# Layer 0 of a two-layer diffusion trunk: tokens and RMS factor first, adaLN scale and shift streamed together, q from the finished input

## The chip, the core and the metric

The kernel runs on one core of a Trainium2 chip. Its engines are TensorE (PE, with its weight loads shown apart as PEld), VectorE (DVE), ScalarE (ACT), GpSimd (POOL) and SyncE (SP), which issues most of the loads. The metric is the time of one execution on the device in microseconds; the median of three runs stands for the kernel. All data are float32; the large products split each operand into a high and a low part of the type fp32r.

## The reference, cut to what matters

Layer 0 takes 384 tokens (128 of a prompt, 256 of a sample) of 2048 features. The two groups have their own condition vector.

```python
def rms_norm(x, g):
    y = x * lax.rsqrt(jnp.mean(x * x, axis=-1, keepdims=True) + EPS)
    return y * g

def adaln(cond, w_mod, b_mod):
    m = jax.nn.silu(cond) @ w_mod + b_mod
    shift, scale, gate = jnp.split(m, 3, axis=-1)
    return shift[:, None, :], scale[:, None, :], gate[:, None, :]

# in reference(), for each layer and each of the two groups
h = rms_norm(x, g) * (1.0 + scale) + shift
proj = h @ w_in          # ga, gb, gate_a, q, k, v, gate_b for layer 0
```

After that, layer 0 runs a conformer branch (a 31-tap convolution over `ga * sigmoid(gb)`, layer norm, SiLU, a gate) beside attention with normed q and k, projects the joined result with `w_out`, multiplies by `gate` and adds it to x. Layer 1 does the like with other branches, and a final RMS norm ends it.

## The kernel before

Features lie on the 128 partitions, in 16 chunks of 128; the tokens lie along the free axis (`xT` is 128 x 16 x 384). The normed and modulated input of a layer is held as `hhi` and `hlo`, each weight tile as `whi` (a cast on ScalarE, line 261) and `wlo` (what the cast left over, on VectorE, line 262). A product is three matmuls, hi by hi, hi by lo and lo by hi. `proj_feat` gives features by tokens (line 354, 384 columns), `proj_tok` and `q_unit` give tokens by features (lines 333 and 571, 512 columns). There are two buffers' worth of room in few places only: three `whi`, three `wlo`, seven raw weight tiles of 512 KB, four slots of 1 MB for the adaLN weights (`ring`), four buffers of the tag `wk` for rows of 384.

The adaLN vectors are products of one row pair with a weight of 2048 x 2048 per part (scale, shift, gate). `gemv_block` loads such a weight in tiles (line 139 holds its matmuls, which write four 32-row strips of one bank); `mod_part` then copies the bank on ScalarE (line 143), transposes it on TensorE (line 172), sums it on VectorE (158), adds the bias (160) and, for the scale, multiplies by the norm's gain (163). With `widths` the scale of layer 0 comes in blocks of 256, 256, 512, 512 and 512 features, that is 2, 2, 4, 4 and 4 chunks.

The first stage of before works so. The blocks of scale are loaded, and with each block the tokens of the same chunks. `make_h` multiplies x by scale only: neither the RMS factor nor the shift is in `hhi` and `hlo` yet. `q_unit` projects q of such a chunk at once. The squares for the RMS factor are summed beside that (`square_sum`, ScalarE and GpSimd), so that the factor `rs0` is there when q is evacuated from PSUM, and is multiplied in there (line 507). The shift is loaded later, four tiles ahead of each quarter of the k and v projection (`shifted`); it makes the finished `hhi` and `hlo` that all later projections read. q misses the shift's share so far. It is added in a bias pass: `wq0` is loaded a second time in 16 half-megabyte tiles, the shift (`sst`) is multiplied with it by `gemv_block`, a selector matmul (line 634) spreads the two rows over the tokens, and VectorE adds the result to q (line 637).

The order of the instructions is made by a scheduler from priorities: `first()` gives the stage's code the highest, `later()` a low one; within an engine the order is fixed at build time and each engine then runs its list in order. SP's list of loads is held in program order by `sync_load`. Work without a place of its own, the remaining adaLN parts and the bias pass, hangs in `gemv_q`; `pump` takes `bg["rate"]` of its tiles after each unit of a projection (R0 until attention, RA after it, RB from the layer norm on).

In the rows, `gv` is the bank of the adaLN products and of the bias pass, `ring` and `raw` are weight tiles, `q`, `pt` and `pf` the banks of q, of the token projections (k and v first) and of the feature projections, `cst` the condition, `gs` the copied bank, `mod` the finished vector, `area` and `mix` scratch rooms for other adaLN parts on VectorE.

Of the kernel before, what the change touches and what calls it, by code (L numbers as in the profile page):

```python
# [19 lines left out]
P = 128  # L20
D = 2048
# [21 lines left out]
R0 = 1.7  # L43
SHIFT_AT = (7, 9, 11)
RA = 1.35
RB = 1.1
# [5 lines left out]
def trunk(ctx: ExitStack, tc: tile.TileContext, d: dict, o: dict):  # L52
# [69 lines left out]
    def gemv_block(w, f0, nf, stat, done):  # L122
# [3 lines left out]
        def unit(u):  # L126
            if u == 0:
                st["ps"] = ps_gv.tile([P, 512], F32, tag="gv", name="gv")
# [12 lines left out]
            if nk * (u + 1) == KC:  # L141
                gs = tmp.tile([P, 512], F32, tag="gs", name="gs", bufs=1)
                nc.scalar.copy(gs[:, :nf], ps[:, :nf])
                done(gs, ps)
# [20 lines left out]
    def mod_part(layer, part, widths=(512, 512, 512, 512), f0=0):  # L165
# [10 lines left out]
        for nf in widths:  # L176
            units += gemv_block(d[f"mod_w{layer}"][4 * part + f0 // 512], f0 % 512, nf, lambda k: cst[:, 2 * k:2 * k + 32],
                                lambda gs, ps, f0=f0, nf=nf: consume(f0, nf, gs, ps))
            f0 += nf
# [319 lines left out]
    def qkv_evacs(v, nat, rs=None):  # L499
        def ev_q(q):  # L500
            def ev(t, ps):
                dst = nat[t][:, 4 * q:4 * q + 4, :]
                src = ps.rearrange("p (h c) -> p h c", h=4)
                if rs is None:
                    nc.scalar.copy(dst, src)
                else:
                    nc.scalar.activation(dst, src, AF.Copy, scale=rs[:, t:t + 1])
# [65 lines left out]

    widths = (256, 256, 512, 512, 512)
    scale_q = mod_part(0, 1, widths)
    pq = [[acc("q0") for t in range(NT)], [acc("q1"), acc("q1"), aux("q1")]]
    av, square = square_sum()
    k0 = 0
    for j, nf in enumerate(widths):
        n = nf // P  # L580
        with first():
            for _ in range(2048 // (2048 // nf * P)):
                scale_q.pop(0)()
            sync_load(xT[:, k0:k0 + n, :], d["xT"][:, k0:k0 + n, :])
            for k in range(k0, k0 + n):
                make_h(0, k)
        last = j == len(widths) - 1
        if last:
            for k in range(k0, KC):
                square(k)  # L590
        for k in range(k0, k0 + n):
            q_unit(k)
            if not last:
                square(k)
            elif k == k0 + 1:
                rs0 = rstd_cols([av], D, "rs0")
                rb0 = rstd_rows(rs0, "rb0")
# [5 lines left out]
    eq0, eq1, ekv = qkv_evacs(v, nat, rs0)  # L603
# [7 lines left out]
    shift_q = mod_part(0, 0)  # L611

    def shifted(u):
        with first():
            for _ in range(4):
                shift_q.pop(0)()
        for k in range(4 * u, 4 * u + 4):
            h = tmp.tile([P, T], F32, tag="wk", bufs=4, name="h32")
            scale_norm(0, h, k, rb0)
            shift_split(0, h, k)  # L620
    proj_tok(d["wkv0"][0], ekv, before=shifted)
# [4 lines left out]
    selb = spare[:, :256].rearrange("p (g c) -> p g c", g=2)  # L626
    side_load(selb, d["selb"])
    sst = spare[:, 1280:1792].rearrange("p (k c) -> p k c", c=32)
    nc.gpsimd.memset(sst, 0.0)
    nc.gpsimd.tensor_copy(sst[:, :, 0:2], mods[0, 0])  # L630
# [343 lines left out]
```

## Time and profile before

| | |
|---|---|
| median of 3 runs | 1300.25 us (1298.58 to 1300.34) |
| span of the profiled execution | 1295.9 us |
| PE busy | 1267.4 us, 98% of the span, 7000 records |
| DVE busy | 882.0 us, 68% |
| ACT busy | 544.5 us, 42% |
| POOL busy | 142.2 us, 11% |
| DMA | 252.76 MB, mean 195 GB/s |

The profiled execution's own time is read as its span, from the first to the last instruction; the runs' times are a little above it. A float32 product (adaLN, transposes of some kinds, attention) appears as more than one record for each instruction of the program, so counts of records and of instructions differ there. Times in the rows are microseconds from the start of the span unless marked ns. A matmul's end is modelled, so TensorE's busy share says less than the number of matmuls in a stretch.

### The profile page before, as it was taken

To read this page: it belongs to the slowest core of one execution; us is meant where nothing else is said; L and a number is where in the kernel's file an instruction comes from. 1 tells how busy PE (TensorE), PEld (TensorE's weight loads), DVE (VectorE), ACT (ScalarE), POOL (GpSimd) and SP (SyncE) were. 2 spreads that over 40 slices of the span, in tenths; PEclk is the share of its full clock that TensorE was granted. 3 is DMA by queue.
4 is the path that set the end of the run, shared out by engine and by line. 5 is a ranking of instruction groups with operands and counts; after the bars stand their busy time and mean duration, and the time that the engine had idled before them with its cause. 6 is when DMAs were issued, how large, how long until landed. Compare 5 with 4: busy or idle time off the path is not lost.

```text
span 1295.9 us, 18150 instructions
## 1 busy us (share of the span) xinstructions
PE 1267.4 (98%) x7000; PEld 1123.1 (87%) x7000; DVE 882.0 (68%) x1464; ACT 544.5 (42%) x941; POOL 142.2 (11%) x162
## 2 busy tenths in 40 slices
PE   6999999999999999999999999999999999999997
PEld 4566687888887888999999988899999999999997
DVE  2245627899999979989976932454544689996443
ACT  3344433644556645432363633344444422343332
POOL 0210100210000042122220000000000011111110
PEclk9999999999999999999999999999999999999998
DMA  9988867688654566676644444433333577764412
GB/s 364 403 309 313 300 185 258 232 307 295 226 166 160 196 221 218 209 225 217 199 135 130 121 128 130 123 118 109 98 99 103 185 231 229 252 194 146 123 50 98
DMA packets 71222, 252.76 MB, mean 195 GB/s; under 512 B 7456, under 2 KB 11808, under 8 KB 67552
## 3 DMA queue, kind: packets, MB, share of 16 engines
q1 hardware_dynamic: 59920, 211.90, 48.9%
q0 software_dynamic: 11072, 39.60, 9.8%
q8 instruction: 55, 0.90, 0.3%
q14 instruction: 31, 0.25, 0.1%
q10 hardware_dynamic: 144, 0.10, 0.0%
HBM read 247.91 MB, written 3.67 MB: 194 GB/s over the span
## 4 chain that ended last, share of the span: by engine, by line
PE 85%; DMA 5%; DVE 5%; issue 3%; POOL 1%; ACT 1%; SPq 0%; DVEq 0%; POOLq 0%; ACTq 0%
PE pf L354 57%; PE pt L333 10%; PE q L571 6%; PE gv L139 5%; DMA area<-in_mod_w 3%; DVE area L197 2%; PE s_ps L470 2%; PE o_ps L495 2%; DVE wlo L262 1%; DMA raw<-in_wf 1%; PE pT_ps L491 1%; DMA ring<-in_mod_w 1%; PE gv L172 1%; POOL lvar L718 1%; PE y_ps L862 1%
## 5 line engine op out<-in xcount | busy, mean ns | idle before, releaser
L354 PE MATMUL pf<-hhi,whi 128*128 128x384 f32 (+1 forms) x1664 | 569.2, 342 | 0.7 <-ACT whi L261 0.7
L354 PE MATMUL pf<-hlo,whi 128*128 128x384 f32 (+1 forms) x1664 | 569.7, 342 | 0.0
L354 PE MATMUL pf<-hhi,wlo 128*128 128x384 f32 (+1 forms) x1664 | 567.2, 343 | 1.7 <-DVE wlo L262 1.7
L262 DVE TENSOR_TENSOR wlo<-raw,whi 128x1024 fp32r<-128x1024 f32 x256 | 314.8, 1230 | 294.3 <-ACT whi L261 288.9
L261 ACT CAST whi<-raw 128x1024 fp32r<-128x1024 f32 x256 | 268.3, 1049 | 466.3 <-PE pf L354 242.5
L354 PEld LDWEIGHTS pf<-hhi,whi 128*128 128x128 f32 x1664 | 313.1, 188 | 24.0 <-issue 14.2
L354 PEld LDWEIGHTS pf<-hhi,wlo 128*128 128x128 f32 x1664 | 313.3, 188 | 9.8 <-issue 3.2
L354 PEld LDWEIGHTS pf<-hlo,whi 128*128 128x128 f32 x1664 | 313.6, 188 | 5.3 <-issue 2.9
L197 DVE SCALAR_TENSOR_TENSOR area<-area,cst 128x512 f32<-128x512 f32 x240 | 177.8, 777 | 14.7 <-DMA area<-in_mod_w 14.5
L659 DVE SCALAR_TENSOR_TENSOR cv<-apad,cw,cv 128x399 f32<-128x399 f32 x240 | 140.6, 635 | 1.1 <-ACT cv L657 0.8
L91 POOL DMA_DIRECT2D area<-in_mod_w x64 | 34.7, 542 | 424.0 <-DVE area L197 222.0
L333 PE MATMUL pt<-wlo,hhi 128*128 128x512 f32 x192 | 75.8, 395 | 0.0
L254 POOL TENSOR_TENSOR sacc<-sacc,sqf 128x384 f32<-128x384 f32 x43 | 55.2, 1284 | 186.9 <-ACT sqf L253 185.1
L333 PE MATMUL pt<-whi,hhi 128*128 128x512 f32 x192 | 75.7, 397 | 0.0
L333 PE MATMUL pt<-whi,hlo 128*128 128x512 f32 x192 | 75.0, 396 | 0.0
L333 PEld LDWEIGHTS pt<-whi,hhi 128*128 128x128 f32 x192 | 36.0, 188 | 12.4 <-ACT hhi L280 2.5
L571 PE MATMUL q<-whi,hhi 128*128 128x512 f32 x96 | 41.1, 428 | 4.4 <-ACT hhi L267 4.4
L478 ACT ACTIVATE pr<-s_ps,nm 128x384 f32<-128x384 f32 (+1 forms) x48 | 24.4, 509 | 49.7 <-DVE nm L477 34.7
L333 PEld LDWEIGHTS pt<-whi,hlo 128*128 128x128 f32 x192 | 36.0, 188 | 10.1 <-issue 0.8
L333 PEld LDWEIGHTS pt<-wlo,hhi 128*128 128x128 f32 x192 | 36.1, 188 | 9.0 <-issue 0.8
L139 PE MATMUL gv<-ring,cst 128*32 128x512 f32 (+1 forms) x288 | 35.8, 582 | 8.2 <-DMA ring<-in_mod_w 7.6
L571 PE MATMUL q<-wlo,hhi 128*128 128x512 f32 x96 | 40.5, 422 | 0.0
(171 smaller groups left out, 991.8 us busy)
## 6 DMA issues: line engine op xcount, KB each, us to landing
raw<-in_wf SPq DMA_DIRECT2D x144, 512.0 KB, 4.5
ring<-in_mod_w SPq DMA_DIRECT2D x32, 1024.0 KB, 7.5
area<-in_mod_w POOLq DMA_DIRECT2D x64, 512.0 KB, 4.6
raw<-in_w_out SPq DMA_DIRECT2D x64, 512.0 KB, 4.4
raw<-in_mod_w SPq DMA_DIRECT2D x56, 512.0 KB, 5.6
raw<-in_wq SPq DMA_DIRECT2D x32, 512.0 KB, 8.8
raw<-in_wt SPq DMA_DIRECT2D x24, 512.0 KB, 3.6
raw<-in_wkv SPq DMA_DIRECT2D x8, 512.0 KB, 7.8
```

What stands on the lines that cost most here:

```text
L91: ins = nc.gpsimd.dma_start(dst, src).ins
L139: nc.tensor.matmul(ps[32 * g:32 * g + 32, :nf], lhsT=stat(k), rhs=raw[:, i % raw.shape[1], :], start=(k < 4), stop=(k >= KC - 4))
L197: nc.vector.scalar_tensor_tensor(av[:, g], raw[:, i], cst[:, 2 * k + g:2 * k + g + 1], av[:, g], ALU.mult, ALU.add)
L254: nc.gpsimd.tensor_tensor(av, av, s, ALU.add)
L261: nc.scalar.copy(dst_hi, src)
L262: order["split"] = nc.vector.tensor_tensor(dst_lo, src, dst_hi.bitcast(F32), ALU.subtract).ins
L333: nc.tensor.matmul(pp[t], lhsT=x[:, k, tt], rhs=y[:, i, :], start=(k == 0 and n == 0), stop=(k == KC - 1 and n == 2))
L354: ins = nc.tensor.matmul(pp[j][:, :n], lhsT=x[:, i, fj], rhs=y[:, k, :n], start=(begin and k % 8 == 0 and m == 0), stop=(end and k % 8 == ...
L470: nc.tensor.matmul(ps, lhsT=mix[:, h0 + h, t * P:(t + 1) * P], rhs=kT[:, kv, c0:c0 + nk * P], start=True, stop=True)
L495: nc.tensor.matmul(po, lhsT=v[:, slots[j], kv * HD:(kv + 1) * HD], rhs=pT[:, j, :], start=(j == 0), stop=(j == nk - 1))
L571: nc.tensor.matmul(pq[b][t], lhsT=x[:, k, tt], rhs=y[:, 0, 512 * b:512 * b + 512], start=(k == 0 and n == 0), stop=(k == KC - 1 and n == 2))
L659: nc.vector.scalar_tensor_tensor(st["o"], apad[:, c, j:j + CVW], cw[:, c, j:j + 1], st["o"], ALU.mult, ALU.add)
```

## The change

All tokens are loaded first, in four loads. `norm_sum` squares them on ScalarE and adds on VectorE; the RMS factor by token (`rb0`) follows at once. Then scale and shift of a block are loaded one after the other through the same four slots, the shift with a PSUM bank (`aux`) and a copy room of its own. `norm_h` makes the finished input of a chunk: x by the factor on GpSimd, scale and shift in one VectorE operation per group, then the split. q is projected from that. The bias pass with its second load of `wq0`, the selector table and `add_bias` is gone, and so are `make_h` and `shifted` from layer 0; q is evacuated by a plain copy. The three rates of the background work are 1.0, 1.0 and 0.8 in place of 1.7, 1.35 and 1.1.

```diff
-R0 = 1.7
+R0 = 1.0
-RA = 1.35
-RB = 1.1
+RA = 1.0
+RB = 0.8
...
+    def norm_sum():
+        av = tmp.tile([P, T], F32, tag="sacc", name="sacc", bufs=1)
+        for c in range(4):
+            sync_load(xT[:, 4 * c:4 * c + 4, :], d["xT"][:, 4 * c:4 * c + 4, :])
+            for k in range(4 * c, 4 * c + 4):
+                if k == 0:
+                    nc.scalar.activation(av, xT[:, k, :], AF.Square)
+                else:
+                    s = tmp.tile([P, T], F32, tag="wk", bufs=4, name="sqx")
+                    nc.scalar.activation(s, xT[:, k, :], AF.Square)
+                    nc.vector.tensor_tensor(av, av, s, ALU.add)
+        return av
+
+    def norm_h(k):
+        h = tmp.tile([P, T], F32, tag="wk", bufs=4, name="h32")
+        nc.gpsimd.tensor_tensor(h, xT[:, k, :], rb0, ALU.mult)
+        for g, c0, c1 in GROUPS:
+            nc.vector.tensor_scalar(h[:, c0:c1], h[:, c0:c1], mods[0, 1][:, k, g:g + 1], mods[0, 0][:, k, g:g + 1],
+                                    ALU.mult, ALU.add)
+        split(hhi[:, k, :T], hlo[:, k, :T], h)
+
     widths = (256, 256, 512, 512, 512)
     scale_q = mod_part(0, 1, widths)
+    shift_q = mod_part(0, 0, widths, bank=lambda: aux("gv_shift"),
+                       row=lambda: big.tile([P, 512], F32, tag="att", name="gs_shift", bufs=3))
     pq = [[acc("q0") for t in range(NT)], [acc("q1"), acc("q1"), aux("q1")]]
-    av, square = square_sum()
+    with first():
+        rb0 = rstd_rows(rstd_cols([norm_sum()], D, "rs0"), "rb0")
     k0 = 0
-    for j, nf in enumerate(widths):
+    for nf in widths:
         n = nf // P
         with first():
-            for _ in range(2048 // (2048 // nf * P)):
-                scale_q.pop(0)()
-            sync_load(xT[:, k0:k0 + n, :], d["xT"][:, k0:k0 + n, :])
+            for q in (scale_q, shift_q):
+                for _ in range(n):
+                    q.pop(0)()
             for k in range(k0, k0 + n):
-                make_h(0, k)
...
+                norm_h(k)
         for k in range(k0, k0 + n):
             q_unit(k)
...
-    shift_q = mod_part(0, 0)
-
-    def shifted(u):
...
-    proj_tok(d["wkv0"][0], ekv, before=shifted)
+    proj_tok(d["wkv0"][0], ekv)
...
-    def add_bias(b, gs, pb):
-        for g, ts in ((0, (0,)), (1, (1, 2))):
-            nc.tensor.matmul(pb, lhsT=selb[:, g, :], rhs=gs, start=True, stop=True)
-            for t in ts:
-                x = nat[t][:, 4 * b:4 * b + 4, :]
-                nc.vector.tensor_tensor(x, x, pb.rearrange("p (h c) -> p h c", h=4), ALU.add)
-    bias_q = [f for b in range(2) for f in
-              gemv_block(d["wq0"][0], 512 * b, 512, lambda k: sst[:, k, :], lambda gs, ps, b=b: add_bias(b, gs, ps))]
...
-    gemv_q.extend(bias_q + mod_part(0, 2) + mod_part(1, 1, (512,) * 3))
+    gemv_q.extend(mod_part(0, 2) + mod_part(1, 1, (512,) * 3))
```

On TensorE before, at the end of the fourth block of scale, the four transposes of the copied bank stand among the q matmuls of the third block (`q_101` and its like are the six banks of q; the last adaLN product stands 22 rows further up):

```order
L571 MATMUL q_101<-whi,hlo 128x512
L571 MATMUL q_102<-whi,hhi 128x512
L172 MATMUL gv<-ident,gs 128x128 x4
L571 MATMUL q_102<-wlo,hhi 128x512
L571 MATMUL q_102<-whi,hlo 128x512
L571 MATMUL q_103<-whi,hhi 128x512
```

On TensorE now, at the end of the second block (`gv_shift` is the shift's bank, `gs_shift` its copy):

```order
L572 MATMUL q_106<-wlo,hhi 128x512
L572 MATMUL q_106<-whi,hlo 128x512
L145 MATMUL gv<-ring,cst 32x512 x4
L145 MATMUL gv_shift<-ring,cst 32x512 x4
L178 MATMUL gv<-ident,gs 128x128 x4
L145 MATMUL gv_shift<-ring,cst 32x512 x4
L145 MATMUL gv_shift<-ring_98,cst 32x512 x4
L145 MATMUL gv_shift<-ring,cst 32x512 x4
L178 MATMUL gv_shift<-ident,gs_shift 128x128 x4
L572 MATMUL q_101<-whi,hhi 128x512
```

The q matmuls of the second block are all ahead of the last adaLN products and of both sets of transposes; the next row of q belongs to the third block. The fourth and the fifth block end in the same way, with the last tile of shift, its transposes, and then q of the next block.

On VectorE before, at the third block, between the sum of the scale's transposes and the first `hlo` of that block:

```order
L158 TENSOR_REDUCE mod_99<-gv 128x8
L160 TENSOR_TENSOR mod_99<-mod_99,vecs 128x8
L262 TENSOR_TENSOR wlo<-raw,whi 128x1024
L163 SCALAR_TENSOR_TENSOR mod_99<-mod_99,vecs 128x8
L262 TENSOR_TENSOR wlo<-raw,whi 128x1024
L268 SCALAR_TENSOR_TENSOR hlo<-xT,mod_99,hhi 128x128
```

On VectorE now, at the same place (`h_456` is the first chunk's x times the factor):

```order
L164 TENSOR_REDUCE mod_99<-gv 128x8
L166 TENSOR_TENSOR mod_99<-mod_99,vecs 128x8
L169 SCALAR_TENSOR_TENSOR mod_99<-mod_99,vecs 128x8
L268 TENSOR_TENSOR wlo<-raw,whi 128x1024 x2
L164 TENSOR_REDUCE mod_100<-gv_shift 128x8
L166 TENSOR_TENSOR mod_100<-mod_100,vecs 128x8
L268 TENSOR_TENSOR wlo<-raw,whi 128x1024
L592 TENSOR_SCALAR h_456<-h_456,mod_99,mod_100 128x128
L592 TENSOR_SCALAR h_456<-h_456,mod_99,mod_100 128x256
```

Two weight splits stand ahead of the shift's sum and one behind it; `hhi` of the chunk, on ScalarE, can only follow the last two rows. On ScalarE the copy into `gs_shift` has one weight cast ahead of it there:

```order
L149 COPY gs<-gv 128x512
L267 CAST whi<-raw 128x1024
L149 COPY gs_shift<-gv_shift 128x512
L267 CAST whi<-raw 128x1024 x2
L267 CAST hhi<-h_456 128x384
```

## Rows read from the trace of the kernel before

**Rows 1.** The page, part 1: busy us, share of the span, records of TensorE.

```profile
PE 1267.4 (98%) x7000; PEld 1123.1 (87%) x7000; DVE 882.0 (68%) x1464; ACT 544.5 (42%) x941; POOL 142.2 (11%) x162
```

**Rows 2.** Windows of 20 us: busy us (records) by engine, PEclk, DMA share, GB/s.

```profile
core 0: us, PE busy (x) PEld busy (x) DVE busy (x) ACT busy (x) POOL busy (x), PEclk, DMA share, GB/s
0.00:20.00 20.00, 9.76 (x48) 5.68 (x49) 4.19 (x12) 6.40 (x12) 1.20 (x5) 1.00 0.96 329
...
280.00:300.00 20.00, 20.00 (x125) 17.35 (x123) 20.00 (x38) 7.60 (x14) 1.25 (x3) 1.00 0.87 296
...
540.00:560.00 20.00, 20.00 (x116) 20.00 (x115) 17.47 (x24) 6.10 (x7) 3.73 (x5) 1.00 0.74 235
```

**Rows 3.** The chain that ended last, in order of time: start, us, what (xrecords).

```profile
14.79 6.46 PE q L571 x18
...
45.65 7.39 PE q L571 x24
...
154.20 0.97 PE pf L354 x4
...
155.61 3.66 PE pf L354 x20
159.26 8.36 PE pt L333 x36
...
364.38 1.72 PE o_ps L495 x4
...
511.26 34.74 PE pf L354 x197
...
736.64 100.45 PE pt L333 x432
```

**Rows 4.** Timeline of 40 to 46 us: TensorE, then ScalarE, then VectorE.

```profile
40.97 1.07 PE L139 MATMUL gv<-ring,cst 128*32 128x512 f32 x8
42.79 0.66 PE L172 MATMUL gv<-ident,gs 128*128 128x128 f32 x4 [0.76 <-ACT gs L143]
45.65 0.50 PE L571 MATMUL q<-whi,hhi 128*128 128x512 f32 x1 [2.20 <-ACT hhi L267]
...
42.15 0.59 ACT L143 COPY gs<-gv 128x512 f32<-128x512 f32 x1 [3.82 <-PE gv L139]
42.63 1.99 ACT L261 CAST whi<-raw 128x1024 fp32r<-128x1024 f32 x2
45.20 2.88 ACT L267 ACTIVATE hhi<-xT,mod 128x128 fp32r<-128x128 f32 x8 [0.57 <-DVE mod L163]
...
43.55 0.19 DVE L158 TENSOR_REDUCE mod<-gv 128x8 f32<-128x32 f32 x1 [3.96 <-PE gv L172]
43.86 1.22 DVE L262 TENSOR_TENSOR wlo<-raw,whi 128x1024 fp32r<-128x1024 f32 x1
45.00 0.16 DVE L163 SCALAR_TENSOR_TENSOR mod<-mod,vecs 128x8 f32<-128x8 f32 x1
```

**Rows 5.** Groups of instructions by line: the bias pass (busy us, mean ns, idle).

```profile
L139 PE MATMUL gv<-raw,mix 128*32 128x512 f32 x64 | 7.9, 600 | 0.0
...
L634 PE MATMUL gv<-gs,mix 128*128 128x512 f32 x8 | 4.3, 618 | 1.2 <-ACT gs L143 0.8 <-DVE nat L637 0.5
...
L637 DVE TENSOR_TENSOR nat<-nat,gv 128x512 f32<-128x512 f32 x6 | 3.9, 678 | 0.0
```

**Rows 6.** Timeline of TensorE from 6 to 10 us: the first two tiles of scale.

```profile
6.61 1.93 PE L139 MATMUL gv<-ring,cst 128*32 128x256 f32 x16 [6.61 <-DMA ring<-in_mod_w]
...
9.49 1.94 PE L139 MATMUL gv<-ring,cst 128*32 128x256 f32 x16 [0.96 <-DMA ring<-in_mod_w]
```

**Rows 7.** Windows of 4 us after the gap, columns as in rows 2.

```profile
44.00:48.00 4.00, 2.35 (x7) 1.92 (x8) 4.00 (x9) 3.43 (x9) 0.00 (x0) 0.81 1.02 424
48.00:52.00 4.00, 4.00 (x15) 3.12 (x14) 0.93 (x3) 0.08 (x1) 0.00 (x0) 0.76 1.00 408
```

**Rows 8.** Groups of instructions by line, ScalarE, VectorE and GpSimd, first stage.

```profile
L261 ACT CAST whi<-raw 128x1024 fp32r<-128x1024 f32 x33 | 34.5, 1049 | 71.0 <-DMA raw<-in_wf 22.8 <-issue 20.7 <-PE pt L333 16.7
...
L253 ACT ACTIVATE sqf<-xT 128x384 f32<-128x384 f32 x15 | 6.7, 511 | 8.9 <-DMA xT<-in_xT 8.9
...
L262 DVE TENSOR_TENSOR wlo<-raw,whi 128x1024 fp32r<-128x1024 f32 x32 | 39.4, 1233 | 90.1 <-ACT whi L261 89.6 <-DMA raw<-in_wq 0.4
...
L254 POOL TENSOR_TENSOR sacc<-sacc,sqf 128x384 f32<-128x384 f32 x43 | 55.2, 1284 | 186.9 <-ACT sqf L253 185.1 <-issue 1.0
```

**Rows 9.** DMA issues from 92 to 99 us: KB each, median us to landing.

```profile
ring<-in_mod_w SPq DMA_DIRECT2D x2, 1024.0 KB, 4.7
```

More of the change, by code (lines that the diff above doesn't have):

```diff
@@ L120, in ring_slot, with gv_bank, gs_row, gemv_block @@
         return ring["slots"][ring["n"] % len(ring["slots"])]
-    def gemv_block(w, f0, nf, stat, done):
+    def gv_bank():
+        return ps_gv.tile([P, 512], F32, tag="gv", name="gv")
+    def gs_row():
+        return tmp.tile([P, 512], F32, tag="gs", name="gs", bufs=1)
+    def gemv_block(w, f0, nf, stat, done, bank=gv_bank, row=gs_row):
         nk = 2048 // nf
@@ L127, in unit @@
             if u == 0:
-                st["ps"] = ps_gv.tile([P, 512], F32, tag="gv", name="gv")
+                st["ps"] = bank()
             ps = st["ps"]
@@ L141, in unit @@
             if nk * (u + 1) == KC:
-                gs = tmp.tile([P, 512], F32, tag="gs", name="gs", bufs=1)
+                gs = row()
                 nc.scalar.copy(gs[:, :nf], ps[:, :nf])
@@ L163, in mod_finish, with mod_part @@
             nc.vector.scalar_tensor_tensor(dst, dst, 1.0, gg, ALU.add, ALU.mult)
-    def mod_part(layer, part, widths=(512, 512, 512, 512), f0=0):
+    def mod_part(layer, part, widths=(512, 512, 512, 512), f0=0, **where):
         if (layer, part) not in mods:
@@ L177, in mod_part @@
             units += gemv_block(d[f"mod_w{layer}"][4 * part + f0 // 512], f0 % 512, nf, lambda k: cst[:, 2 * k:2 * k + 32],
-                                lambda gs, ps, f0=f0, nf=nf: consume(f0, nf, gs, ps))
+                                lambda gs, ps, f0=f0, nf=nf: consume(f0, nf, gs, ps), **where)
             f0 += nf
@@ L497, in attend, with qkv_evacs @@
         nc.scalar.copy(mix[:, h0:h0 + 4, t * P:(t + 1) * P], po.rearrange("p (h c) -> p h c", h=4))
-    def qkv_evacs(v, nat, rs=None):
+    def qkv_evacs(v, nat):
         def ev_q(q):
             def ev(t, ps):
[L502 to L507, printed above, removed]
+                nc.scalar.copy(nat[t][:, 4 * q:4 * q + 4, :], ps.rearrange("p (h c) -> p h c", h=4))
             return ev
@@ L610, in trunk @@
     order["hold"] = None
-    shift_q = mod_part(0, 0)
-    def shifted(u):
[L614 to L620, printed above, removed]
-    proj_tok(d["wkv0"][0], ekv, before=shifted)
+    proj_tok(d["wkv0"][0], ekv)
     ring["slots"] = []
@@ L952, in _tables @@
     tri = np.stack([np.where(j <= i, 0.0, -1e30), np.where(j >= i, 0.0, -1e30)], axis=1).astype(f)
-    sel = np.zeros((P, 2), f)
-    for g in range(4):
-        sel[32 * g, 0] = 1.0
-        sel[32 * g + 1, 1] = 1.0
-    selb = np.repeat(sel[:, :, None], P, axis=2)
-    return {"selb": np.ascontiguousarray(selb), "ident": np.eye(P, dtype=f), "rope": np.ascontiguousarray(rope), "tri": np.ascontiguousarray(tri)}
+    return {"ident": np.eye(P, dtype=f), "rope": np.ascontiguousarray(rope), "tri": np.ascontiguousarray(tri)}
 def kernel(**inputs):
```

16 lines of the change are left out of this document (1 added, 15 removed).

## The prediction

> **What bounds the kernel now.** I read the page's engine lines first: TensorE is busy for 98% of the span [rows 1]. A busy matmul row proves little, so I went to the windows of 20 us and looked at counts. A stretch with nothing but feature projections holds some 114 to 116 matmuls per 20 us [rows 2], and the chain of waits gives the pace: 197 of them in 34.74 us, 0.176 us each, and 432 of 512 columns in 100.45 us, 0.2325 us each [rows 3]. Against that pace TensorE loses time in few places: the first 20 us do little (48 matmul records [rows 2]), one gap stands at 42 us, and there are short waits around the bias pass. So the kernel is bound by TensorE from about 15 us on; a removed matmul is worth its length, and a gap in the first stage costs its length. VectorE comes next: it is full in stretches of the convolution, 20.00 of 20 us in the window from 280 [rows 2].
>
> The one gap of the first stage is the pattern that the change multiplies. The last product of a block of adaLN scale ends at 40.97 + 1.07 = 42.04; ScalarE copies it (0.59), TensorE transposes (0.66), VectorE sums and adds, with a weight split of 1.22 in between, ScalarE makes the first hhi, and the next q matmul starts at 45.65 [rows 4]: 3.6 us from product to q. The later blocks of before have no such gap because the order puts the transposes among q matmuls of the block before.
>
> **What is removed.** The bias pass goes: 64 matmul records of 7.9 us, eight selector records of 4.3 us, and 1.2 us of waiting in front of them [rows 5]: 13.4 us, all on TensorE and so all on the path. Its bounds: 11.3 if the eight selector records run at the pace of other float32 products of 512 columns (four in 1.72 us [rows 3]) and the waits stay in some other form, 14.6 if each of the twelve groups also gives back the tenth of a us that a return to other work costs. I take 13.4, the busy time read for just these rows. What else goes with it is cover for nothing: 16 loads of wq0 (the DMA engines are not full there), six VectorE adds, two ScalarE copies, a Pool memset and a selector load on Pool's queue. The adds are 3.9 us [rows 5]; VectorE has that much slack in the convolution, so I take 0, with 3.9 of gain as the other end.
>
> **What the front costs.** Before, q starts at 14.79 [rows 3]: two tiles of scale must land. Now 3.15 MB of tokens and four tiles (two of scale, two of shift) must land first. Tiles with runs of 1 KB land 2.9 us apart (TensorE is released at 6.61 and 9.49 [rows 6]); everything else moves at 408 to 424 GB/s [rows 7], so 2.5 us per 1 MB tile, 1.27 per half, 7.6 for the tokens. Counting 3.7 us for the first byte (6.6 less 2.9): tokens at 11.3, fourth tile at 22.9. From the second tile to the first q took 14.79 - 9.49 = 5.3 us before; the new chain has two more VectorE operations (scale and shift of 128 and of 256 columns). No row of before shows them; by the nearest ones they cost between 0.3 (two of the 0.16 of 128x8 [rows 4]) and 1.2 together (one of 1.23 for 1024 columns [rows 8]); I take 0.7, so 22.9 + 5.3 + 0.7 = 28.9. The RMS factor is hidden: squares at 0.51 us each on ScalarE follow the tokens [rows 8], their 15 adds on VectorE run beside them, and the factor is there by about 20. Pool's 16 products of x and the factor (1.28 us each by the adds of the same shape [rows 8]) are hidden as well, as long as they stay ahead of the shift.
>
> The Trainium skill, "DMA: Bandwidth & Descriptors", section Specifications, gives 512 B as the smallest transfer that runs at line rate. By it the four tiles would land at 2.5 us each and the sum below would be about 1.6 us lower, at 1304.9; the trace does not agree (2.9).
>
> **The blocks.** Chunks of q come in blocks of 2, 2, 4, 4, 4. A q matmul is 0.2325, a tile's products 1.1 (1.07 and a little at the return [rows 4]), a set of transposes about 0.5. The new order puts the last shift product of a block behind all q matmuls that are left, then the transposes, then q of the next block, so nothing covers the chain.
> Block 1: 36 q 8.4, five tiles 5.5, transposes 0.4, and 2.3 for the slow start (18 matmuls took 6.46 and not 4.2 [rows 3]): 28.9 + 16.6 = 45.5.
> Block 2: 8.4 + seven tiles 7.7 + 0.5, and 1.8 of waiting for the last two shift tiles: their slots are held by scale tiles whose products stand behind 25 to 36 q, and a lone load lands 4.7 us after its issue [rows 9]. 63.9.
> Boundary to block 3: the copy of the last product stands behind a weight cast (1.05 [rows 8]) whose load lands 1.3 us after the last tile, and two weight splits stand ahead of VectorE's sum, one behind it (1.23 each [rows 8]). 3.6 + 1.3 + 1.8 = 6.7. 70.6.
> Block 3: 72 q 16.7, eight tiles 8.8, 0.5, and 1.8 for a slow clock (24 matmuls in 7.39 and not 5.6 after the gap of before [rows 3]): 98.4. Boundary: the cast ahead of the copy waits for the last q of the block, so part runs under the last product: 2.7. 101.1.
> Block 4: 26.0, then a boundary like that of before plus one VectorE operation, 4.0: 131.1. Block 5: 16.7 + 1.8, then 144 kv matmuls, 33.5: 183.1.
> Before, kv ends at 159.26 + 8.36 = 167.62, with 24 feature matmuls (4.2 us) already done [rows 3]: 163.4 on the same count of work. The stage loses 19.7 us. Its bounds: 2 us if only the front stays, 27 if each boundary costs the 6.7 of the first.
>
> After kv the same matmuls follow, fewer background tiles before the layer norm and four more behind it, at the same price on TensorE. Sum: 19.7 - 13.4 = +6.3 us. The span read is 1295.9, the median of the runs 1300.25; the 4.35 between them stays: **1306.5 us**.
>
> **The clock.** In 44 to 48 us the granted clock was 0.81, in 48 to 52 0.76 [rows 7]: part of each at 1.2 GHz instead of 2.4, after TensorE had waited 3.6 us save for four transposes. I charge this twice, at the long boundaries, 1.8 each.
>
> **Rivals.** *Short boundaries, faster.* If the splits and casts at the boundaries are done early, a boundary is only copy and transpose (0.59 + 0.66), the clock stays high, and no slot is waited for: 6.3 - (13.4 - 3.7) - 1.8 - 3.6 = -8.8, 1291.5. Without clock and slot losses it decides at 3.3 us a boundary: below that the kernel is faster. For it: later blocks of before show no gap at all. Against: the order leaves no q to cover them. 0.12.
> *Even.* Boundaries of 3.6 as seen before, the clock low once, a little of the slot wait: 1306.5 - 2.6 - 1.8 - 1 = 1301, so 1298 to 1302.8. For it: the 6.7 rests on where one weight load lands. 0.20.
> *Forecast.* 1306.5, in 1302.9 to 1313. 0.46.
> *The clock falls at every boundary.* Then block 2 and block 4 start slow too, at 1.8 each as after the gap of before [rows 3]: 1310. For it: TensorE also waits inside block 2, so that the stretch around it is thin. Against: before the second block of before there was no such fall. 0.15.
> The Trainium skill, "TensorE: Matmul & The Clock Gate", section "HAM oscillation — how this bites in real kernels", says that bursts of matmuls with waits between them restart at the low clock each time; it speaks against this change and is this rival, and the one gap of the trace bears it out.
> *The bias gain does not arrive.* If VectorE and not TensorE sets the pace of the convolution (it is full in one window [rows 2]), the 13.4 us fall into its shadow: up to 1320. Against: TensorE is full there too, and VectorE loses the adds and the rotary work from that stretch. 0.07.
>
> **How the numbers follow.** A change within 0.2% (2.6 us) is about what a measurement of this kernel cannot tell from none. Slower: forecast, clock and lost gain, 0.68; same 0.20; faster 0.12. The range 1296 to 1314 leaves out most of the faster rival (about 0.1) and the upper part of the last (about 0.06).
>
> **What would show it.** In the profile after: first q at 28 to 30 us; TensorE gaps of 2 to 7 us ahead of the first q of the third, fourth and fifth block, each ended by ScalarE's hhi, with the clock below 1 behind at least one; kv ending near 183; no L634 or mix products and no gap at 200 to 220; from then on the same pace as before. The forecast is wrong if kv ends before 177 (the boundaries are short) or if TensorE's waits for wlo or conv grow after 200 us (VectorE binds).

## The result and the profile after

The changed kernel takes 1308.2 us (median of 4 runs, 1306.52 to 1309.06) against 1300.3 of the kernel before, run beside it. The ratio on record is 1.0070, with a 95% interval of 1.0055 to 1.0084; the two medians alone give 1.0061. It is slower, by 7.9 us by the medians and 9.1 by the ratio, where 6.3 was forecast (1306.5). The time came out near the forecast, and in part by luck: two terms of the sum were off, one by 7.2 us and the other by 3.1 the opposite way, and the reading of the kernel before was off by another 2.6.

The engine line of the page, which answers [rows 1]: TensorE has 40 records fewer and is busy for 4.6 us less in a span that is 11 us longer.

```profile
PE 1262.8 (97%) x6960; PEld 1124.3 (86%) x6960; DVE 873.2 (67%) x1427; ACT 526.4 (40%) x890; POOL 136.3 (10%) x160
```

Windows of 20 us, as in [rows 2]: from 60 to 80 us TensorE is busy for 11.46 us only, and the granted clock is 0.74 there. The last window of [rows 2], 540 to 560 us, has the same 116 matmuls as before.

```profile
0.00:20.00 20.00, 5.04 (x38) 2.63 (x38) 9.28 (x22) 8.98 (x19) 1.06 (x5) 1.00 0.95 330
20.00:40.00 20.00, 16.37 (x120) 9.34 (x116) 6.88 (x14) 4.62 (x8) 6.08 (x6) 0.91 1.08 366
60.00:80.00 20.00, 11.46 (x61) 5.45 (x54) 8.57 (x20) 6.09 (x9) 4.32 (x4) 0.74 1.01 407
```

The chain of waits, which answers [rows 3] (start, us, what). The first q of each block stands at 29.03, 47.84, 74.05, 105.97 and 138.30, k and v run from 156.82 to 190.30, and k and v of layer 1 start at 746.96.

```profile
29.03 4.39 PE q L572 x12
...
47.84 6.03 PE q L572 x25
...
60.26 7.36 DMA raw<-in_wq
...
74.05 4.91 PE q L572 x12
...
105.97 4.37 PE q L572 x12
...
138.30 18.51 PE q L572 x72
156.82 33.48 PE pt L339 x144
...
746.96 100.45 PE pt L339 x432
```

What TensorE waited for between 20 and 160 us, in us, number of times and the longest: 19.3 us in 11 waits, the first q's among them.

```profile
PE q L572 <- ACT hhi L267: 12.5, 5, 3.7
PE gv_shift L178 <- ACT gs_shift L149: 3.7, 4, 1.8
PE gv_shift L145 <- DMA ring<-in_mod_w: 3.1, 2, 2.4
```

The longest boundary, ahead of the third block, on the timeline of TensorE, ScalarE and VectorE (it answers [rows 4]). The last shift tile is late (2.39 us of waiting); its copy waits behind the cast of a weight that has only just landed; two splits run ahead of VectorE's sum and one behind it; `hhi` follows, and q starts 6.6 us after the last product's end (66.39 + 1.06 = 67.45).

```profile
66.39 1.06 PE L145 MATMUL gv_shift<-ring,cst 128*32 128x512 f32 x8 [2.39 <-DMA ring<-in_mod_w]
67.64 1.04 ACT L267 CAST whi<-raw 128x1024 fp32r<-128x1024 f32 x1 [7.12 <-DMA raw<-in_wq]
68.59 0.58 ACT L149 COPY gs_shift<-gv_shift 128x512 f32<-128x512 f32 x1
68.72 1.23 DVE L268 TENSOR_TENSOR wlo<-raw,whi 128x1024 fp32r<-128x1024 f32 x1 [6.76 <-ACT whi L267]
...
71.29 0.18 DVE L164 TENSOR_REDUCE mod<-gv_shift 128x8 f32<-128x32 f32 x1
...
71.60 1.22 DVE L268 TENSOR_TENSOR wlo<-raw,whi 128x1024 fp32r<-128x1024 f32 x1
72.73 2.40 DVE L592 TENSOR_SCALAR h<-h,mod,mod 128x128 f32<-128x128 f32 x8
73.48 2.25 ACT L267 CAST hhi<-h 128x384 fp32r<-128x384 f32 x4 [2.13 <-DVE h L592]
...
74.05 0.79 PE L572 MATMUL q<-whi,hhi 128*128 128x512 f32 x1 [3.71 <-ACT hhi L267]
```

Windows of 4 us behind the five places at which q starts (PEclk is the third figure from the end; they answer [rows 7]). The clock is down behind the first q and behind the third, fourth and fifth block's, and full behind the second's.

```profile
28.00:32.00 4.00, 2.97 (x10) 2.36 (x11) 3.03 (x7) 1.03 (x2) 1.36 (x2) 0.80 1.09 348
...
48.00:52.00 4.00, 4.00 (x18) 3.25 (x19) 0.94 (x2) 0.37 (x1) 2.35 (x2) 1.00 1.02 422
72.00:76.00 4.00, 1.95 (x5) 1.57 (x6) 4.00 (x12) 2.05 (x4) 0.32 (x1) 0.50 1.01 426
104.00:108.00 4.00, 2.07 (x6) 1.65 (x6) 3.73 (x14) 2.05 (x4) 0.40 (x1) 0.68 1.02 424
140.00:144.00 4.00, 4.00 (x13) 3.18 (x12) 1.26 (x3) 0.00 (x0) 0.00 (x0) 0.62 0.09 35
```

The two profiled executions side by side, on the prediction's count of work (k and v before end at 163.4 if the 24 feature matmuls that are done by then are taken off): the first stage loses 190.30 - 163.4 = 26.9 us; from there to layer 1's k and v it was 736.64 - 163.4 = 573.2 [rows 3] and is 746.96 - 190.30 = 556.7, a gain of 16.5; the rest loses 0.6. That is 11.0 on the span. The medians differ by less, 7.9. In every run whose span is listed the time is 1.7 to 1.9 us above the span; by that the profiled execution of before took an estimated 1297.6 us, some 2.6 below the median of its runs.

### The profile page after: what moved, and what is told of

Read it like the earlier page. It is cut to its first block, busy times and chain, and to the rows that moved or that the text cites. A ratio compares the mean times of both kernels' runs of the same rounds, so it can differ in the third digit from the quotient of the medians.

```text
span 1306.9 us, 17957 instructions
## 1 busy us (share of the span) xinstructions
PE 1262.8 (97%) x6960; PEld 1124.3 (86%) x6960; DVE 873.2 (67%) x1427; ACT 526.4 (40%) x890; POOL 136.3 (10%) x160
## 4 chain that ended last, share of the span: by engine, by line
PE 93%; DVE 2%; DMA 2%; issue 1%; ACT 1%; SPq 0%; POOL 0%; DVEq 0%; ACTq 0%; POOLq 0%
PE pf L360 65%; PE pt L339 10%; PE q L572 6%; PE gv L145 4%; PE s_ps L476 2%; PE o_ps L501 2%; DVE area L203 1%; PE pT_ps L497 1%; PE gv_shift L145 1%; DMA ring<-in_mod_w 1%; PE gvt L211 1%; DVE wlo L268 1%; DMA raw<-in_wq 1%; PE y_ps L853 1%; PE qT_ps L462 0%
## 5 line engine op out<-in xcount | busy, mean ns | idle before, releaser
L203 DVE SCALAR_TENSOR_TENSOR area<-area,cst 128x512 f32<-128x512 f32 x240 | 175.3, 768 | 19.3 <-DMA area<-in_mod_w 19.2
L260 POOL TENSOR_TENSOR sacc<-sacc,sqf 128x384 f32<-128x384 f32 x28 | 34.7, 1239 | 131.6 <-ACT sqf L259 129.1
L572 PEld LDWEIGHTS q<-whi,hhi 128*128 128x128 f32 x96 | 20.0, 209 | 23.3 <-ACT hhi L267 14.6
```

The costliest lines, as they stand in the source:

```text
L203: nc.vector.scalar_tensor_tensor(av[:, g], raw[:, i], cst[:, 2 * k + g:2 * k + g + 1], av[:, g], ALU.mult, ALU.add)
L260: nc.gpsimd.tensor_tensor(av, av, s, ALU.add)
L572: nc.tensor.matmul(pq[b][t], lhsT=x[:, k, tt], rhs=y[:, 0, 512 * b:512 * b + 512], start=(k == 0 and n == 0), stop=(k == KC - 1 and n == 2))
```

## Experiments

Each gives its median and, in brackets, its ratio to the kernel before as run beside it, with the 95% interval. The changed kernel stands at 1308.2 (1.0070). The kernel before had medians from 1297.4 to 1300.3 beside the experiments, so 2 or 3 us between the medians of two experiments say little by themselves; the ratios compare better.

### What the first stage waits for

**More slots.** The ring gets two more slots, made of two half-size rooms each.

```diff
-    ring["slots"] = [ring_a[:, 0], ring_a[:, 1], ring_a[:, 2], ring_b[:, :2048]]
+    half = [big.tile([P, n], F32, tag=tag, name="half", bufs=b)[:, :1024]
+            for tag, n, b in (("kT", 1024, 1), ("v", 1024, 1), ("att", 1280, 3), ("att", 1280, 3))]
+    ring["slots"] = [[ring_a[:, 0]], [ring_a[:, 1]], [ring_a[:, 2]], [ring_b[:, :2048]], half[:2], half[2:]]
```

> The changed kernel with six slots for the adaLN tiles of the first stage in place of four (two more out of rooms that stand empty there). Theory: the 12 us without q ahead of the third block come from shift tiles whose loads wait for slots, while the DMA engines stand nearly idle from 52 to 56 us; with six slots q of the third block starts 5 to 8 us earlier (74.05 now, 66 to 69), and the end of k and v and the time follow: 1300 to 1304. Rival: the stage is bound by the bytes of scale, shift and tokens; the loads that are freed there wait later, k and v end within 2 us of 190.3, and the time stays at 1306 to 1309.

Measured: 1308.8 (1.0079, 1.0062 to 1.0096). The third block's q starts at 70.66 and not at 74.05, so the wait for slots was real; by the fifth block nothing is left of it (138.24 against 138.30), and k and v start at 156.5. The rival is right on the time. One reason is in TensorE's timeline of this version: products of a tile that arrives in halves are issued apart, and a half takes TensorE as long as a whole tile.

```profile
117.34 1.07 PE L147 MATMUL gv<-ring,cst 128*32 128x512 f32 x8
118.22 1.03 PE L147 MATMUL gv<-half,cst 128*32 128x512 f32 x4
```

So the slots were tried at a price of their own, and what whole slots would give stays open. The wait of 4.2 us ahead of the fifth block, from product to q, did not change at all: it is the chain, and no slot can help it.

**No shift loads.** The shift's products read the scale's tiles.

```diff
-            slot = ring_slot()
+            slot = None if share is not None and share["take"] else ring_slot()
...
+            if share is not None and "take" in share and share["take"]:
+                raws = share["q"].pop(0)
```

> The changed kernel with the shift's products reading the scale's tiles, so that 16 MB of loads go (the shift is left out of the computation: it takes the scale's weights). All products, transposes and chains stay. Theory (the bytes of the shift are what the first stage waits for): first q at 22 to 24 us instead of 29.0, k and v start at 122 to 134 instead of 156.6, the time 1276 to 1286. Rival (the chains at the block boundaries and the slow clock behind them cost it, loads or not): first q 6 us earlier, the rest of the stage as long as now: 1300 to 1303.

Measured: 1287.6 (0.9909, 0.9894 to 0.9924). k and v start at 136.1, 20.8 us earlier than in the changed kernel. The start and the time stand just outside the theory's ranges (122 to 134, 1276 to 1286). The first q was not earlier at all (30.3): the chain to it no longer begins with a tile but with the additions for the RMS factor (the last one from 16.21 to 16.78), runs through the products that spread the factor (until 25.06), and has one tile of the second block in it (1.00 us). Two things change at once here, the loads and the order, since the scheduler covers the boundaries with q when it believes the tiles to be there: the last 145 q matmuls run in one piece.

```profile
102.47 33.59 PE q L576 x145
```

**A shorter last block.**

```diff
-    widths = (256, 256, 512, 512, 512)
+    widths = (256, 256, 512, 512, 256, 256)
```

> The changed kernel with the last block of four chunks cut into two blocks of two (widths 256, 256, 512, 512, 256, 256). Theory (the stage is bound by the DMA stream, and the q left after the last tile is its tail): the tail halves from 72 to 36 q matmuls, 8.4 us less, eight tiles with runs of 1 KB cost 0.5 us more each, 4 us, and the last boundary is partly covered by q: k and v end 4 to 7 us earlier, 1301 to 1304.5. Rival (each boundary costs its chain, whatever the stream does): one boundary more, 3 to 4 us slower: 1311 to 1312.5.

Measured: 1304.35 (1.0041, 1.0026 to 1.0056); k and v start at 151.9, 4.9 us earlier. The theory's size is right. Its words are only half of the cause: in this order the transposes of the last two blocks stand among q matmuls again, so that the wait ahead of the fifth block is gone and the one ahead of the sixth is 1.59 us; and the granted clock, 0.62 from 140 to 144 us in the changed kernel, is 1.00 from 130 to 150 here.

**Eight blocks of two chunks.**

```diff
-    widths = (256, 256, 512, 512, 512)
+    widths = (256,) * 8
```

> The changed kernel with eight blocks of two chunks (widths 256 throughout). Theory: what the stage waits for is the arrival of a whole block of scale and shift, 8 MB for a wide block (the third block waited 14 us from the last scale product to q) and 4 MB for a narrow one; with narrow blocks the stream of loads runs through, four tiles of 3.0 us and two weight tiles of 1.27 us per block, 14.5 us, and after the last tile only 36 q matmuls are left: k and v start at 141 to 145 instead of 156.6, the time is 1293 to 1298. Rival: each of the seven boundaries costs the chain from the last product to q, 3.5 us and a slow clock behind it, and the tiles with runs of 1 KB cost 0.5 us more each: 1306 to 1313.

Measured: 1299.8 (1.0015, 1.0005 to 1.0024), k and v from 147.5 on. Between theory and rival, and almost the time of the kernel before. q of the blocks starts every 15.05 us, near the 14.5 that I had given to the loads, and the DMA engines are full. That looked like a stage paced by loads.

**The same, laid out by block.** Scale and shift lie in memory block by block, so that a tile of 256 columns is read in runs of 8 KB; the instructions and their order stay.

```diff
+    for part in range(2):
+        f0 = 2048 * part
+        for b, nf in enumerate(WIDTHS):
+            out[f"ms{part}_{b}"] = a["mod_w0"][:, f0:f0 + nf].reshape(KC, P, nf).transpose(1, 0, 2)
```

> The version with eight blocks of two chunks (1299.8), with scale and shift of layer 0 laid out in memory block by block, so that a tile of 256 columns is read in runs of 8 KB and not of 1 KB; instructions and their order are the same. Theory (that version's stage is paced by the loads: q of the blocks started every 15.05 us, four tiles of 3.0 and two weight tiles of 1.27 are 14.5): tiles land 2.5 us apart, a block takes 13.0 to 13.6 us, where TensorE's own work of a block is 13.2; first q at 26 to 27, k and v start at 131 to 137 instead of 147.3, the time 1284 to 1290. Rival (the boundary's chain paces it, not the loads): first q at 26 to 27, the period stays near 15: 1296.5 to 1299.

Measured: 1299.3 (1.0009, 1.0000 to 1.0017). The theory falls; the rival's mechanism holds, and its time is missed by 0.3 us. The first q came at 29.3, not at 26 to 27 as both had it. Tiles do land 2.5 us apart at the front (14.66, 17.16, 19.65 and 22.16), and the DMA engines are no longer full in the blocks; the period is 15.05 us again. Windows of 30 us of the two versions, eight blocks before and after the new layout (DMA share and GB/s are the last two figures):

```profile
90.00:120.00 30.00, 27.50 (x207) 17.51 (x208) 11.28 (x28) 7.47 (x13) 4.70 (x4) 1.00 1.07 357
```

```profile
90.00:120.00 30.00, 27.20 (x213) 17.01 (x206) 11.82 (x28) 7.70 (x13) 4.70 (x4) 1.00 0.96 357
```

TensorE itself sets the period. Its timeline at a boundary of the version laid out by block shows how: two waits of 0.49 and 0.91 us, between product and transpose and between transpose and q, with one tile's products as the only cover.

```profile
89.21 1.07 PE L146 MATMUL gv_shift<-ring,cst 128*32 128x256 f32 x16
90.78 0.44 PE L179 MATMUL gv_shift<-ident,gs_shift 128*128 128x128 f32 x2 [0.49 <-ACT gs_shift L150]
91.15 1.07 PE L146 MATMUL gv<-ring,cst 128*32 128x256 f32 x16
93.13 0.50 PE L574 MATMUL q<-whi,hhi 128*128 128x512 f32 x1 [0.91 <-ACT hhi L269]
```

36 q matmuls are 8.4 us, four tiles at 1.2 with the return to other work 4.8, the transposes some 0.5, the two waits 1.4: 15.1.

**A first block of one chunk.**

```diff
-WIDTHS = (256,) * 8
+WIDTHS = (128, 128) + (256,) * 7
```

> As the version with blocks laid out in memory, with the first block of two chunks cut into two of one chunk (widths 128, 128, then 256). Theory (the stage is bound by TensorE once tiles land 2.5 us apart, so what is gained at the front is kept): first q 4 to 5 us earlier than with eight blocks of 256, at 21.5 to 23, and the time 2 to 4 us lower than that version's. Rival (the loads bound it even so): same time within 1.5 us of the version with eight blocks.

Measured: 1305.0 (1.0056, 1.0043 to 1.0069). Both miss. The first q starts at 28.7 all the same: products of the second block's scale stand ahead of the first block's last transpose (1.35 us), and the products that spread the RMS factor end only at 23.45. The second block's q starts at 43.4 and the third's, the first of two chunks, at 53.7.

**The chain covered by q.** The version laid out by block, with the last 15 q matmuls of a block held back.

```diff
+            q_part(k, hi, lo, bts[6 - hold:6 - 3], product)
+            q_part(k, hi, lo, bts[6 - 3:], transpose)
...
+                if after is not None:
+                    tc.add_manual_dep(ins, after.name, NOSYNC, reason="cover the next block's chain")
```

> The version with eight blocks laid out in memory (1299.3), with the last 15 q matmuls of each block held behind the next block's last shift product, nine of them behind its transposes, so that q covers the chain from product to transpose and from transpose to the first q of the next block. Theory: that version's period of 15.05 us is TensorE's own order, 36 q of 0.2325 (8.4), four tiles of 1.2, transposes 0.7, and two uncovered waits of 0.46 and 0.88 us; without the waits the period is 13.7 to 14.2, k and v start at 138 to 142 instead of 147.9, and the time is 1290.5 to 1294.5. Rival: with the products standing closer together the four slots come free later and the loads set the period, 14.5 to 15.5: 1297 to 1301.

Measured: 1287.9 (0.9925, 0.9912 to 0.9938), the fastest that leaves nothing out, 0.75% below the kernel before and below the theory's range. The period falls to 13.67 us and k and v start at 136.8. Six q cover the copy, nine and a tile cover the chain to `hhi`; the wait ahead of the transposes is gone, and 0.38 to 0.42 us remain ahead of the first q of the third to seventh block, 1.59 ahead of the last one's. The granted clock, which is 0.91 and 0.92 from 130 to 140 and 140 to 150 us in the version without the hold, stays at 1.00 here once it is back behind the first q.

```profile
94.27 1.07 PE L146 MATMUL gv_shift<-ring,cst 128*32 128x256 f32 x16
...
96.77 0.38 PE L179 MATMUL gv_shift<-ident,gs_shift 128*128 128x128 f32 x2
...
99.18 1.07 PE L146 MATMUL gv<-ring,cst 128*32 128x256 f32 x16
100.64 0.51 PE L572 MATMUL q<-whi,hhi 128*128 128x512 f32 x1 [0.39 <-ACT hhi L269]
```

The DMA share is 0.98 in this version (90 to 120 us), and with runs of 1 KB it was already 1.07 at a period of 15.05; four tiles of 3.0 and two of 1.27 would by themselves take 14.5. So the new layout is probably needed as well; held q without it was not run.

### What the bias pass was worth

**Old rates.** The changed kernel with 1.7, 1.35 and 1.1.

```diff
-R0 = 1.0
+R0 = 1.7
-RA = 1.0
-RB = 0.8
+RA = 1.35
+RB = 1.1
```

> The changed kernel with the three rates of the background work as before (1.7, 1.35, 1.1). Theory: the rates move adaLN tiles between stages at the same price on TensorE; the time stays within 1.5 us of the changed kernel, 1306.7 to 1309.7. Rival: the lower rates are what shortened the waits around the layer norm (4.3 us of lost TensorE time at 480 to 520 before, 2.6 after), so that the old rates give 2 to 3 us back: 1310 to 1311.5.

Measured: 1308.7 (1.0076, 1.0059 to 1.0092). The theory holds: the rates are worth nothing that can be told from zero (0.06% by the ratios, with intervals of some 0.15% to either side).

**TensorE's part put back.** Products, copies and spreading products of the bias pass run again in the changed kernel.

```diff
+    def spread(gs, pb):
+        for _ in range(2):
+            nc.tensor.matmul(pb, lhsT=ident, rhs=gs, start=True, stop=True)
+    bias_q = [f for b in range(2) for f in gemv_block(d["wq0"][0], 512 * b, 512, lambda k: cst[:, 2 * k:2 * k + 32], spread)]
-    gemv_q.extend(mod_part(0, 2) + mod_part(1, 1, (512,) * 3))
+    gemv_q.extend(bias_q + mod_part(0, 2) + mod_part(1, 1, (512,) * 3))
```

> The changed kernel with TensorE's part of the bias pass put back where it stood, at the head of the background work: 16 loads of wq0, their products, two copies and two products of 128x512 each; the result is used by nothing. Prices the pass's TensorE time in the changed kernel. Theory (TensorE sets the pace behind k and v): +12 to +14 us, 1320 to 1322.5. Rival (VectorE sets the pace from the first convolution tap to the layer norm, as it did when the pass alone was taken out of the kernel before, which gained 6.6 us): +3 to +8 us, 1311 to 1316.

Measured: 1321.7 (1.0173, 1.0154 to 1.0192), 13.5 more than the changed kernel by the medians, 13.4 by the ratios. In the chain the stretch between the two k and v projections is 763.18 - (158.37 + 33.48) = 571.3 us, 14.6 more than the changed kernel's 556.7. So the 13.4 us that the prediction read from the rows is near what the pass costs there. Not all of it is the pass's own work: TensorE's waits in that stretch are 3.0 us against 0.8 in the changed kernel, and the granted clock is down once (0.96 from 480 to 520 us, 1.00 in the changed kernel).

```profile
158.37 33.48 PE pt L339 x144
763.18 36.96 PE pt L339 x159
```

**More for VectorE.** Twelve additions of 128x512 in the convolution.

```diff
+        if fb in (0, 1, 2):
+            for _ in range(4):
+                junk = tmp.tile([P, 512], F32, tag="gs", name="junk", bufs=1)
+                nc.vector.tensor_tensor(junk.rearrange("p (a c) -> p a c", a=4), ident.unsqueeze(1).broadcast_to([P, 4, P]),
+                                        ident.unsqueeze(1).broadcast_to([P, 4, P]), ALU.add)
```

> The changed kernel with twelve more VectorE additions of 128x512 (four behind each of the first three pairs of feature tiles, some 0.6 to 0.7 us each, 7 to 8 us in all); the result is used by nothing. Theory (TensorE sets the pace, VectorE has slack in the convolution): within 1.5 us of the changed kernel, 1306.7 to 1309.7. Rival (VectorE sets the pace between the first tap and the layer norm, which comes as much later as VectorE has more to do): +5 to +8 us, 1313 to 1316.

Measured: 1318.0 (1.0161, 1.0138 to 1.0184), 9.8 more by the medians and 11.8 by the ratios for 8.1 us of VectorE; its runs lie between 1315.8 and 1323.2. The theory falls, and the rival was too low. VectorE's groups between the first tap and the layer norm's factor, of this version and then of the changed kernel:

```profile
L203 DVE SCALAR_TENSOR_TENSOR area<-area,cst 128x512 f32<-128x512 f32 x28 | 24.1, 900 | 2.7 <-DMA area<-in_mod_w 2.6
...
L680 DVE TENSOR_TENSOR junk<-ident 128x512 f32<-128x512 f32 x12 | 8.1, 677 | 0.0
```

```profile
L203 DVE SCALAR_TENSOR_TENSOR area<-area,cst 128x512 f32<-128x512 f32 x14 | 13.7, 1023 | 1.4 <-DMA area<-in_mod_w 1.4
```

The factor itself, on TensorE's timeline, of this version and of the changed kernel: 508.11 is 319.3 us behind the end of k and v, 487.50 only 297.2.

```profile
508.11 0.83 PE L226 MATMUL rsl<-ones,lvar 128*128 128x1 f32 x6
```

```profile
487.50 0.83 PE L226 MATMUL rsl<-ones,lvar 128*128 128x1 f32 x6 [0.58 <-POOL lvar L709]
```

The factor comes 22.1 us later. The additions are 8.1 us of that, and the new order let 14 more `area` operations of the next layer's shift in ahead of the layer norm, 10.4 us more. Which of the two costs what was not taken apart. What TensorE pays shows in its waits between the two projections of k and v: 7.4 us here, all for VectorE, and 0.8 in the changed kernel. The granted clock is down once as well (0.96 from 480 to 520 us).

```profile
PE gvt L211 <- DVE mod L213: 3.6, 3, 1.8
PE rbl L240 <- DVE diag L239: 2.0, 1, 2.0
PE pf L360 <- DVE wlo L268: 1.8, 2, 1.4
```

**The pass alone taken out of the kernel before.**

```diff
-    gemv_q.extend(bias_q + mod_part(0, 2) + mod_part(1, 1, (512,) * 3))
+    gemv_q.extend(mod_part(0, 2) + mod_part(1, 1, (512,) * 3))
```

> The kernel before without the bias pass and with nothing in its place, so q lacks the shift's share (that part of the computation is left out). Prices the pass by itself. Theory: 13.4 us, the TensorE time of its rows: 1286.9, within 1285.5 to 1289. Rival: 16 to 17 us, as the stages behind k and v gained between the two traces (before: 569 us from the end of k and v to the start of layer 1's k and v on the same count of work; after: 16.6 less): 1283.5 to 1284.5. Rival: VectorE sets the pace of the convolution and the gain is lost: above 1295.

Measured: 1292.1 (0.9955, 0.9938 to 0.9971), 6.6 us less: half of what the same TensorE work cost when it was put back, and none of the three forecasts. The seven runs lie between 1289.4 and 1297.3, and the profiled one is the slowest, so its trace shows less of the gain than the median does. In it the factor of the layer norm comes at 486.67, no earlier than before (484.00), although VectorE is rid of the pass's additions; between the first tap and the factor stand 27 `area` operations, 11 before.

```profile
L197 DVE SCALAR_TENSOR_TENSOR area<-area,cst 128x512 f32<-128x512 f32 x27 | 24.5, 943 | 0.6 <-DMA area<-in_mod_w 0.6
```

**And with those operations held.** Their side loads wait for the last convolution tap.

```diff
+    order["hold"] = order["tap"]
     shifts += [mod_vector(1, 0, j, sums[j - 1][:, :1024], vring) for j in (1, 2, 3)]
+    order["hold"] = None
```

> The kernel before without the bias pass (q lacks the shift's share) and with the side loads of the next layer's shift vectors, rooms of the name area, held until the last convolution tap. Taking the pass out alone gave 1292.1, 6.6 us less, and not the 13 to 15 us of TensorE time that putting it back into the changed kernel cost. Theory: the missing half went to VectorE: in that kernel 34 of the area operations stand ahead of the layer norm's factor, 19 in the kernel before and 20 in the changed one, so the layer norm came no earlier; with 20 of them there the pass is worth its TensorE time: 1283 to 1286.5. Rival: the area operations only fill idle time, and the gain stays at 5 to 8 us: 1290.5 to 1293.5.

Measured: 1290.6 (0.9943, 0.9931 to 0.9955), in the rival's range. The factor comes 13 us earlier, at 473.72, with 13 `area` operations between the first tap and it (the expectation's 34, 19 and 20 count up to about the factor's spreading over the partitions, 6 to 7 us later), and the time barely follows. The theory falls as the whole account. A wait has only moved: in this version TensorE is short of work from 480 to 520 us, and the granted clock is 0.96 there.

```profile
480.00:520.00 40.00, 36.16 (x196) 35.14 (x195) 38.46 (x65) 20.42 (x32) 7.02 (x8) 0.96 0.57 187
```

The changed kernel has 225 matmul records in that window, at a clock of 1.00. Between the two projections of k and v TensorE waits 9.0 us in the version without the pass and 5.4 with the operations held, against 6.2 in the kernel before and 0.8 in the changed one: without the pass alone, the waits do not go. Why the pass's removal pays in full in the one kernel and by half in the other is not settled beyond that. The order around attention differs between them (its first row maximum on VectorE comes 76 us behind the end of k and v in the kernel without the pass, 97 in the changed one); that this is the cause was not tried.

## The prediction, step by step

- **First q**, 28.9: 29.03, with two errors that cancel. Tiles land at 14.83, 17.84, 20.85 and 23.85, 3.0 us apart (2.9 in the sum), the last one 0.95 late; from the start of its products to q it took 5.1 us (23.90 to 29.03) and not the 6.0 of the sum.
- **Block 1**, to 45.5: 47.84. The step that failed is that block 2 was given no boundary: its chain leaves 0.9 us uncovered (the q at 47.84 waits that long for `hhi`). One of its shift tiles was also issued in three pieces (42.01, 43.43 and 44.41), some 1 us more than in one.
- **Boundary to block 3**, 6.7: 6.6, by the steps named, though not at their sizes: the load lands 1.3 us after the last tile (67.62 and 66.35), but most of that runs under the product, and against the 3.6 of before the copy behind the cast costs 1.0, the second split ahead of the sum 0.9. The other 1.1 the sum did not name there: transposes at the low clock (1.11 us, 0.66 before) and the two operations of `norm_h` (0.7). The wait for slots ahead of it, 1.8, was 3.1.
- **Boundaries to blocks 4 and 5**, 2.7 and 4.0: 3.3 (102.68 to 105.97) and 4.2 (134.08 to 138.30).
- **The clock.** Charged three times, 2.3, 1.8 and 1.8; it fell four times. Twelve q matmuls took 4.39, 4.91 and 4.37 us where 2.79 is the pace, and the last 72 took 18.51, not 16.7: 1.6, 2.1, 1.6 and 1.8. The one I left out, behind the boundary to block 4, is the rival's "at every boundary"; behind the short wait of block 2 it did not fall (1.00 from 48 to 52 us). The Trainium skill's section "HAM oscillation — how this bites in real kernels" ("TensorE: Matmul & The Clock Gate") says that bursts with waits between them come back at the low clock; four of the five places agree with it.
- **The stage**, a loss of 19.7: 26.9, at the upper bound of 27, though not by the long boundaries that the bound assumes. The boundaries, taken one by one, were nearly right; the excess is the second block's chain and its split tile, slots, a fourth slow start, and products that cost 1.2 and not 1.1 us among q.
- **The bias pass**, 13.4: the step holds for TensorE (13.5 by the medians when put back). But the stretch behind k and v gained 16.5, and the step that failed is "VectorE has that much slack in the convolution, so I take 0". TensorE was waiting for VectorE there. Its waits between the two projections of k and v were 6.2 us before, 1.3 of them in the pass itself, and are 0.8 now. The three longest of those outside the pass, and then all that are left:

```profile
PE pf L354 <- DVE wlo L262: 1.7, 1, 1.7
PE gvt L205 <- DVE mod L207: 0.9, 1, 0.9
PE rbl L234 <- DVE diag L233: 0.9, 1, 0.9
```

```profile
PE rsl L226 <- POOL lvar L709: 0.6, 1, 0.6
PE rbl L240 <- DVE diag L239: 0.2, 1, 0.2
```

So the term put at nothing is 4.1 us of waits outside the pass (4.9 before, 0.8 now), 3.3 of them for VectorE. With the 12.2 us of the pass's products and its own waits of 1.3 that is 17.6, near the 16.5. What relieved VectorE is not singled out. The six additions are 3.9 us; and since q is ready earlier, some 11.6 us of norm gain and rotary work on q and k (lines 405 to 441 of the kernel before), which stood between the first tap and the layer norm's factor, now stand ahead of the first tap. Neither was put back alone.

- **The rates**, not priced: nothing, as measured.
- **From span to median.** I carried over 4.35 us; the changed kernel's profiled run took 1308.63 at a span of 1306.9, 1.7 more. The other 2.6 were the profiled execution of before lying low among its runs (the estimate above). A stage 7.2 worse, a gain 3.1 better, 0.6 at the end, and this 2.6 and 0.4 the other way make the 1.7 us between 1306.5 and 1308.2. The time is closer than the working deserves, and that is luck.
- **Rivals.** "Short boundaries" needed the chain covered; the version with held q matmuls, which also has narrow blocks and the new layout, does that and lands 0.75% below the kernel before, where the rival had 8.8 us. The threshold given there is mis-added: without the 3.6 of the clock and the 1.8 of the slots, 0.9 us is left with three boundaries at 13.4 together, so it decides at 4.2 us a boundary and not at 3.3. "The bias gain does not arrive" was wrong for this change, and half right for the kernel before without the pass.

The sentence on the smallest transfer that runs at line rate (the Trainium skill, "DMA: Bandwidth & Descriptors", section Specifications) would make tiles with runs of 1 KB and of 8 KB equal; they land 3.0 and 2.5 us apart here, so the measurement decides against it for runs of 1 KB.

## What to carry to other kernels

A product that must go through a copy, a transpose and a small sum before others can use it needed 3.3 to 4.2 us here; leave work of the block before behind its last product, and say so to the scheduler, or each block pays the wait and, as behind three of the four boundaries here, a slow clock. When two engines are both nearly full in a stretch, as here, work given to either moves the end, and a scheduler may fill the space with work that could have waited: read which operations stand ahead of the stretch's end, not only how many us were removed. Before a stage is called bound by its loads, make the loads faster and see whether the period moves.

## What was not expected of the hardware

- The products of half a tile (two of 128x512 in float32, on two strips of 32 columns) take 1.05 us, those of a whole tile (four, on four strips) 1.07.
- Tiles of 1 MB in runs of 1 KB keep the DMA engines at a share of 1.07 to 1.09 for 344 to 364 GB/s; in runs of 8 KB they moved 419 and 423 GB/s at 1.02 (10 to 30 us).
- While GpSimd multiplied x by the factor (22.30 to 26.17 us of the changed kernel), two VectorE operations of 128x4 took 0.98 and 0.92 us (from 24.26 and 25.27); the next one like them, at 26.30 with GpSimd idle, took 0.16. The version laid out by block shows the same three times (0.89, 0.92 and 0.84). No run here tells why.
